# Half-size pieces of the conditioning weights in tiles of their own, and the scaling of the differential outputs on VectorE

## The chip, the cores and the metric

The kernel runs on one core of one Trainium2 chip. The metric is the device time of an execution in microseconds (us); smaller is better. Several runs are timed, and one execution per kernel is recorded by the hardware profiler, from which every duration here comes. Engine names are those of the profile: PE is TensorE (PEld its weight load), DVE is VectorE, ACT is ScalarE, POOL is GpSimd, and SP is the engine that issues most of the loads.

## What is computed

One layer of a diffusion backbone, in fp32, over 256 latent and 256 context tokens with 2048 channels. Cut to what matters here:

```
m_lat = split(silu(c)     @ w_ada + b_ada, 6)          # shift, scale, gate, ... each of 2048
m_ctx = split(silu(c_ctx) @ w_ada + b_ada, 6)
hc = rms_norm(ctx, norm1_g) * (1 + m_ctx[1]) + m_ctx[0]
h  = rms_norm(x,   norm1_g) * (1 + m_lat[1]) + m_lat[0]
ka, va, kb, vb = split(hc @ w_in[:, :KV]), split(h @ w_in[:, :KV])   # keys and values, both streams
qa, qb, ga, gb = split(h @ w_in[:, KV:])                             # queries and gates, latent only
oa = gqa(rope(norm(qa)), ka, va)                       # 16 heads of 128
a  = softmax(q1 k1) - lam * softmax(q2 k2)             # differential attention, 8 heads
ob = rms_norm(a @ vb, subln_g) * (1 - lam_init)
x  = x + m_lat[2] * ((sig(ga) * (oa @ w_br_a) + sig(gb) * (ob @ w_br_b)) @ w_out)
out = x + gate * swiglu(modulated norm of x)           # with w_ff_gate, w_ff_up, w_ff_down
```

## The kernel before

Every large product is made in three matmuls, because fp32 operands are split into a high and a low part. Weights come in tiles of 512 KB (two k-tiles of 128 by 512 columns; `load_w`, DMA at L224) into the pool tag "wraw" of 7 buffers. ACT casts a tile to its high part (`whi`, L235), DVE subtracts that from the tile for the low part (`wlo`, L237), and TensorE then does high x high, high x low and low x high (L241, L242, L243 in `mm3`). All these loads stand in the queue of SP, one behind the other: a DMA that must wait for its tile to become free holds up every one behind it.

The first stage makes keys and values. It walks over the 16 k-tiles in steps (first k-tile, number of k-tiles): (0,1), (1,1), (2,2), (4,4), (8,4), (12,4). In each step, `kv_group` multiplies six column groups of weights with the modulated tokens of that step (`xT` latent, `cT` context) and adds the result to accumulators on DVE (L442) or ACT.

Before a step can start, `ada_cond(k0, nk)` must have made its shift and scale: two parts (shift, then scale), each a product of the conditioning vectors (`cst`) with 16 k-tiles of columns of the conditioning weights `ada_t`. These come in pieces, each of 512 KB: for steps of four k-tiles 8 pieces a part, of two k-tiles each. Each part is 16 matmuls (L314; in fp32 a row of the profile counts 32 records), and its pieces are named `wada`. The pieces of a part go to different places: for all steps of four, the first two go to the halves of one large tile (L299), the next two are loaded as half-size pieces of 256 KB (L303), each into a scratch tile, one with the tag "nr" (2 buffers) and one with the tag "p" (4 buffers); the last four go to wraw tiles (L294). All 16 matmuls of a part run as one group, in reverse order of the pieces. After it a copy, a transposition (`atp`, L324) and small DVE operations make shift and scale, and `modulated` turns the tokens `tok_t` (loaded at L170) into `xT` and `cT` (L356 to L360 on DVE and ACT).

The generator yields inside `ada_cond` and the others mark where work of different kinds is interleaved; the order within an engine follows from the order in which the program issues, and the scheduler keeps an issued order where `tc.issue_after` asks for it.

The rotary tables are made on POOL by `tables` (L198): 32 small multiplications from the loaded tiles `cs` and `used`, which have the tag "p" too. In the first stage ACT and DVE also serve the next conditioning values (`ada` on DVE, L457 and L459, from loads `wada` at L452).

In the attention stage (about 390 to 620 us in the profile), the units of the differential attention come in 16 calls. For each, TensorE makes the output `o` (L835), ACT copies it to SBUF (`on`, L836), makes its sum of squares (L839), DVE scales the sum to a mean (`rstdo`, L123), POOL takes the power -1/2 (L124), and ACT scales `on` by it (L842). One generator step later TensorE transposes it (`otp`, L845), and ACT writes it out (L846). Between these stand the casts and subtractions of weights for the query and gate columns.

Of the kernel before, what the change touches and what calls it, by code (L numbers as in the profile page):

```python
# [11 lines left out]
F32 = mybir.dt.float32  # L12
# [5 lines left out]
P = 128  # L18
# [28 lines left out]
def hybrid_block(ctx: ExitStack, tc: tile.TileContext, t: dict, out: bass.AP):  # L47
# [161 lines left out]
        nc.vector.tensor_scalar(out=neglam, in0=neglam, scalar1=-LAM_INIT, scalar2=None, op0=ALU.add)  # L209


    last_hi, last_lo = [], []

    def load_raw(r0, c0, n=2):
        raw = wp.tile([P, WK, CG], F32, tag="wraw", bufs=WRAW, name="wraw")
# [5 lines left out]

    def load_w(src, r0, c0, nk=WK, in_big=False):
        raw = wp.tile([P, WK, CG], F32, tag="wraw", bufs=WRAW, name="wraw")
        nc.sync.dma_start(out=raw[:, 0:nk], in_=src[r0:r0 + nk * P, c0:c0 + CG].rearrange("(k p) c -> p k c", p=P))  # L224
        return split_w(raw, nk, in_big)

    def split_w(raw, nk, in_big=False, late=None):
# [52 lines left out]
    def ada_cond(k0, nk):  # L280
        ncol = nk * P
        kk = 2 * CG // ncol
        n0 = k0 * P * 2 * D // (P * 2 * CG)
        mod = []
        for part in range(2):
            aps = s_ps("ada")
            held = []
            for q in range(0, NKT, kk):
                piece = t["ada_t"][n0].rearrange("p (k c) -> p k c", c=ncol)
                n0 += 1  # L290
                n = q // kk
                if nk < 4 or n > 3:
                    wt = wp.tile([P, 2 * CG], F32, tag="wraw", bufs=WRAW, name="wada").rearrange("p (k c) -> p k c", c=ncol)
                    nc.sync.dma_start(out=wt, in_=piece)  # L294
                elif n < 2:
                    if n == 0:
                        two = big_tile("wada2").rearrange("p (n k c) -> p n k c", n=2, c=ncol)
                    wt = two[:, n]
                    nc.sync.dma_start(out=wt, in_=piece)  # L299
                else:  # L300
                    wt = [scratch("wada1", tag=tag, bufs=b) for tag, b in (("nr", 2), ("p", 4))]
                    for j in range(2):
                        nc.sync.dma_start(out=wt[j], in_=piece[:, j, :])  # L303
                held += [(q + j, wt[j] if nk == 4 and 1 < n < 4 else wt[:, j, :]) for j in range(kk)]
                last = q + kk == NKT
                if k0 and not last:
                    if nk == 4 and n == 3:
                        yield None
                    continue
                for k, rhs in held[::-1] if k0 else held:  # L310
                    g = k % 4
                    early, late_k = k < 4, k >= NKT - 4
                    with tc.issue_after(last_pe[0].ins) if k0 == 1 and k == held[-1][0] else nullcontext():
                        last_pe[0] = nc.tensor.matmul(aps[32 * g:32 * g + 32, 0:ncol], lhsT=cst[:, k, :], rhs=rhs,  # L314
                                                      start=late_k if k0 else early, stop=early if k0 else late_k)
                held = []
                if last:
                    asb = scratch("asb")
                    last_asb.append(nc.scalar.copy(out=asb[:, 0:ncol], in_=aps[:, 0:ncol]))
                yield None  # L320
                if last:
                    atp = tp_ps("atp")
                    for j in range(nk):
                        nc.tensor.transpose(out=atp[:, j * P:(j + 1) * P], in_=asb[:, j * P:(j + 1) * P], identity=ident)  # L324
                    m = small(f"mod{part}", 8)
                    mv = m[:, 0:2 * nk].rearrange("p (j w) -> p j w", w=2)
                    nc.vector.tensor_reduce(
                        out=mv, in_=atp[:, 0:ncol].rearrange("p (j g m) -> p j m g", g=4, m=32)[:, :, 0:2, :],
                        axis=AX.X, op=ALU.add)
                    nc.vector.tensor_tensor(out=mv, in0=mv,  # L330
                                            in1=bada[:, part * NKT + k0: part * NKT + k0 + nk].unsqueeze(2).to_broadcast([P, nk, 2]), op=ALU.add)
                    mod.append(mv)
        shift, scale = mod
        nc.vector.scalar_tensor_tensor(out=scale, in0=scale, scalar=1.0,
                                       in1=g1[:, k0:k0 + nk].unsqueeze(2).to_broadcast([P, nk, 2]), op0=ALU.add, op1=ALU.mult)
        cond_of[k0] = (shift, scale)
# [465 lines left out]
    def back(br, u, pr):  # L802

        grp, hh = unit(br, u)
        if br == "a":
            if hh % 2 == 0:
                pair[:] = [big_tile("pT", F32R).rearrange("p (k c) -> p k c", k=4) for _ in range(2)]
            pT = list(pair)
        else:
            pT = scratch("pT", tag="pTb", bufs=2).rearrange("p (k c) -> p k c", k=4)  # L810
        for i, p in enumerate(pr):
            tp = tp_ps("ptp")
            for kt in range(4):
                nc.tensor.transpose(out=tp[:, kt * P:(kt + 1) * P], in_=p[:, kt * P:(kt + 1) * P], identity=ident)  # L814
            src = tp.rearrange("p (k q) -> p k q", k=4)
            if br == "a":
                c0 = hh % 2 * SEQ + i * P
                split(*[x[:, :, c0:c0 + P] for x in pT], src)
            else:
                nc.scalar.copy(out=pT, in_=src)  # L820
        yield None
        if br == "a" and hh % 2 == 0:
            return
        op = tp_ps("o")
        if br == "a":
            for kt in range(4):
                vh, vl = [v[:, kt, grp * AD:(grp + 1) * AD] for v in v_a]
                mm3(op, vh, vl, pT[0][:, kt, :], pT[1][:, kt, :], kt == 0, kt == 3)
            last_o.append(nc.scalar.copy(out=o_raw(grp * 4 + hh - 1, 2), in_=op))
            return  # L830
        vb = acc["vb"][grp].rearrange("p (t c) -> p t c", c=CG)
        tk = u % 2
        on = scratch("on", BV, tag="on", bufs=2)
        for kt in range(4):
            nc.tensor.matmul(op[:, 0:BV], lhsT=pT[:, kt, :], rhs=vb[:, kt, hh * BV:(hh + 1) * BV], start=(kt == 0), stop=(kt == 3))  # L835
        nc.scalar.copy(out=on, in_=op[:, 0:BV])  # L836
        junk = scratch("junk_o", tag="sq", bufs=2)
        ss = small("sso", 1)
        nc.scalar.activation(out=junk[:, 0:BV], in_=on, func=AF.Square, accum_out=ss)  # L839
        r = rstd_of(ss, 1, BV, "rstdo")  # L840
        yield None
        nc.scalar.mul(out=on, in_=on, mul=r)  # L842
        yield None
        tp = tp_ps("otp")
        nc.tensor.transpose(out=tp[:, 0:P], in_=on, identity=ident)  # L845
        nc.scalar.mul(out=o_raw(AH + grp * 4 + hh)[:, tk * P:(tk + 1) * P], in_=tp[:, 0:P], mul=gsub)  # L846
# [335 lines left out]
```

## Time and profile before

| | |
|---|---|
| median of 3 runs | 1704.09 us (1702.79 to 1705.93) |
| the profiled execution | 1703.83 us, span 1701.7 us |
| clock granted to TensorE, mean | 0.997 |
| TensorE busy | 1676.8 us, 99% of the span |
| DVE, ACT, POOL busy | 67%, 46%, 12% |
| DMA | 413.08 MB, 243 GB/s on average |

How to read it: a row of a timeline has the start in us, the duration, the engine, the line, the operation, output <- input, and in brackets for how long the engine was idle before it and which engine's instruction (with its line) ended the wait. Matmuls are pipelined: the distance of their starts counts, not their length. A row of the windows has the window, its length, the busy time and the number of instructions of PE, PEld, DVE, ACT and POOL, then the clock granted to TensorE (1.00 is full speed), the share of DMA and GB/s. In the waits, the numbers are the total in us, how many times, and the longest. In the chain of waits a row has start, length and what ran; "SPq" is the issue of a DMA by SP. A row for one line has the shortest, median and longest duration in ns, and the first and last start.

### The profile page before, as it was taken

The page shows a single profiled execution, that of the slowest core. Times are in us where ns is not written, and L with a number is a line of the kernel's source. Part 1 is how long each engine was busy: PE and PEld are TensorE (multiplying, and loading weights), DVE is VectorE, ACT ScalarE, POOL GpSimd, SP SyncE. Part 2 cuts the span into 40 slices and gives each one's busy share as a digit, 9 for nine tenths or more (in the row PEclk, how much of TensorE's full clock was granted, in tenths as well). Part 3 has the DMA queues.
Part 4 walks back from the last instruction along what each step waited for, and adds up shares of the span by engine and source line. Part 5 has one row for each costly group of instructions (what it writes and reads, how often), then busy time and mean ns, then how long its engine had stood idle before and what let it go on. Part 6 is the DMA issues. An engine that isn't in the chain of part 4 may idle for free.

```text
span 1701.7 us, 21519 instructions
## 1 busy us (share of the span) xinstructions
PE 1676.8 (99%) x7889; PEld 1355.1 (80%) x7889; DVE 1138.4 (67%) x1438; ACT 779.0 (46%) x1071; POOL 209.3 (12%) x296
## 2 busy tenths in 40 slices
PE   7999999999999999999999999999999999999998
PEld 5677778887887778888888888888888888888887
DVE  5665779798687878996666755566666666554454
ACT  5221222246666656577544534444444444333332
POOL 0200002011231210011111101111111111100000
PEclk9999999999999999999999999999999999999999
DMA  9787875778766768776777857788888888766662
GB/s 352 288 316 275 304 253 157 234 252 256 246 180 216 222 225 272 246 238 212 256 265 237 294 175 221 235 263 267 263 272 263 269 274 253 238 218 195 216 207 88
DMA packets 181860, 413.08 MB, mean 243 GB/s; under 512 B 15065, under 2 KB 16298, under 8 KB 181498
## 3 DMA queue, kind: packets, MB, share of 16 engines
q1 hardware_dynamic: 169482, 374.17, 67.3%
q0 software_dynamic: 12272, 37.53, 7.4%
q8 instruction: 62, 1.02, 0.3%
q14 instruction: 44, 0.36, 0.1%
HBM read 395.35 MB, written 16.29 MB: 242 GB/s over the span
## 4 chain that ended last, share of the span: by engine, by line
PE 75%; issue 10%; DVE 6%; DMA 4%; POOL 3%; ACT 2%; SPq 0%; POOLq 0%; DVEq 0%; ACTq 0%
PE mm L241 22%; PE mm L242 22%; PE mm L243 22%; DVE wlo L237 2%; PE ada L314 1%; POOL fturn L1091 1%; ACT whi L235 1%; PE ptp L814 1%; DMA turn_d<-fpart 1%; DMA fturn<-turn_d 1%; DMA wraw<-in_w_in_dram 1%; DVE ada L459 1%; PE mm L401 1%; PE o L835 1%; DVE mx L736 1%
## 5 line engine op out<-in xcount | busy, mean ns | idle before, releaser
L237 DVE TENSOR_TENSOR wlo<-wraw,whi 128x1024 fp32r<-128x1024 f32 x498 | 606.8, 1220 | 443.9 <-ACT whi L235 442.9
L235 ACT CAST whi<-wraw 128x1024 fp32r<-128x1024 f32 x498 | 522.4, 1050 | 714.0 <-PE mm L243 607.2
L242 PE MATMUL mm<-wlo,hT 128*128 128x512 f32 x684 | 266.3, 389 | 0.1
L243 PE MATMUL mm<-whi,hT 128*128 128x512 f32 x684 | 266.1, 389 | 0.0
L241 PE MATMUL mm<-whi,hT 128*128 128x512 f32 x684 | 266.1, 389 | 0.0
L241 PE MATMUL mm<-whi,xT 128*128 128x512 f32 x630 | 252.7, 402 | 1.3 <-ACT xT L359 1.2
L242 PE MATMUL mm<-wlo,xT 128*128 128x512 f32 x630 | 247.0, 392 | 4.3 <-DVE wlo L237 4.3
L243 PE MATMUL mm<-whi,xT 128*128 128x512 f32 x630 | 246.9, 392 | 0.0
L459 DVE SCALAR_TENSOR_TENSOR ada<-wada,vt,ada 128x1024 f32<-128x1024 f32 x120 | 152.0, 1277 | 0.0
L242 PEld LDWEIGHTS mm<-wlo,hT 128*128 128x128 f32 x684 | 128.4, 188 | 27.7 <-DVE wlo L237 0.9
L241 PEld LDWEIGHTS mm<-whi,hT 128*128 128x128 f32 x684 | 128.4, 188 | 26.7
L243 PEld LDWEIGHTS mm<-whi,hT 128*128 128x128 f32 x684 | 128.4, 188 | 26.5
L241 PEld LDWEIGHTS mm<-whi,xT 128*128 128x128 f32 x630 | 118.6, 188 | 32.7 <-issue 7.0
L242 PEld LDWEIGHTS mm<-wlo,xT 128*128 128x128 f32 x630 | 118.8, 189 | 28.2 <-DVE wlo L237 5.7
L243 PEld LDWEIGHTS mm<-whi,xT 128*128 128x128 f32 x630 | 118.5, 188 | 26.0 <-DVE xT L360 0.3
L241 PE MATMUL mm<-whi,fT 128*128 128x512 f32 x354 | 137.5, 388 | 0.5 <-DVE y L1127 0.5
L242 PE MATMUL mm<-wlo,fT 128*128 128x512 f32 x354 | 137.3, 388 | 0.0
L243 PE MATMUL mm<-whi,fT 128*128 128x512 f32 x354 | 137.3, 388 | 0.0
L241 PEld LDWEIGHTS mm<-whi,fT 128*128 128x128 f32 x354 | 66.4, 188 | 15.0 <-issue 0.8
L243 PEld LDWEIGHTS mm<-whi,fT 128*128 128x128 f32 x354 | 66.5, 188 | 13.8
L242 PEld LDWEIGHTS mm<-wlo,fT 128*128 128x128 f32 x354 | 66.4, 188 | 13.7
L241 PE MATMUL mm<-whi,oT 128*128 128x512 f32 x192 | 75.9, 396 | 0.0
(236 smaller groups left out, 2150.4 us busy)
## 6 DMA issues: line engine op xcount, KB each, us to landing
wraw<-in_w_in_dram SPq DMA_DIRECT2D x159, 512.0 KB, 4.7
wada<-in_w_ada_dram SPq DMA_DIRECT2D x128, 512.0 KB, 4.6
wraw<-in_w_ff_gate_dram SPq DMA_DIRECT2D x88, 512.0 KB, 4.6
wraw<-in_w_ff_up_dram SPq DMA_DIRECT2D x88, 512.0 KB, 5.4
wraw<-in_w_ff_down_dram SPq DMA_DIRECT2D x88, 512.0 KB, 4.8
wada<-in_ada_t_dram SPq DMA_DIRECT2D x52, 512.0 KB, 7.8
wraw<-in_w_br_a_dram SPq DMA_DIRECT2D x32, 512.0 KB, 5.3
wraw<-in_w_out_dram SPq DMA_DIRECT2D x32, 512.0 KB, 5.2
```

What stands on the lines that cost most here:

```text
L235: last_hi.append(nc.scalar.copy(out=hi[:, 0:nk], in_=raw[:, 0:nk]))
L237: last_lo.append(nc.vector.tensor_tensor(out=lo[:, 0:nk], in0=raw[:, 0:nk], in1=hi[:, 0:nk].bitcast(F32), op=ALU.subtract))
L241: nc.tensor.matmul(ps, lhsT=ah, rhs=wh, start=first, stop=False, skip_group_check=skip)
L242: nc.tensor.matmul(ps, lhsT=ah, rhs=wl, start=False, stop=False, skip_group_check=skip)
L243: return nc.tensor.matmul(ps, lhsT=al, rhs=wh, start=False, stop=last, skip_group_check=skip)
L314: last_pe[0] = nc.tensor.matmul(aps[32 * g:32 * g + 32, 0:ncol], lhsT=cst[:, k, :], rhs=rhs, start=late_k if k0 else early, stop=early if ...
L401: last_pe[0] = nc.tensor.matmul(ps[cg], lhsT=x, rhs=ws0[cg][y], start=(n == 0), stop=(n == 2))
L459: nc.vector.scalar_tensor_tensor(out=dst, in0=wt, scalar=sc[:, 0, kt:kt + 1], in1=dst, op0=ALU.mult, op1=ALU.add)
L736: nc.vector.tensor_reduce(out=mx, in_=sp, axis=AX.X, op=ALU.max, negate=True)
L814: nc.tensor.transpose(out=tp[:, kt * P:(kt + 1) * P], in_=p[:, kt * P:(kt + 1) * P], identity=ident)
L835: nc.tensor.matmul(op[:, 0:BV], lhsT=pT[:, kt, :], rhs=vb[:, kt, hh * BV:(hh + 1) * BV], start=(kt == 0), stop=(kt == 3))
L1091: nc.gpsimd.dma_start(out=whole[32 * b:32 * b + 32].rearrange("p (k a j) -> p k a j", k=4, a=4), in_=blocks[b])
```

## The change

Three things are changed. First, in step (4,4) all eight pieces of a part go to wraw tiles, and its 16 matmuls run as two groups: the pieces of the first half (k-tiles 0 to 7) as soon as they are there, those of the second half behind them. Second, in steps (8,4) and (12,4) the half-size pieces go to scratch tiles with the tags "nr" twice, "sq" and "pTb" (2 buffers each), and no longer to "p"; the DMAs of all pieces of these steps are ordered behind the last weights' load issued before. That is an order, not a wait for the load to land. Third, the scaling of `on` is a tensor_scalar of DVE (L843 of the changed kernel) and no longer an activation of ACT (L842). From L314 on, line numbers of the changed kernel are one higher.

```diff
-    last_hi, last_lo = [], []
+    last_hi, last_lo, last_load = [], [], []
...
     def load_w(src, r0, c0, nk=WK, in_big=False):
...
-        nc.sync.dma_start(out=raw[:, 0:nk], in_=src[r0:r0 + nk * P, c0:c0 + CG].rearrange("(k p) c -> p k c", p=P))
+        last_load.append(nc.sync.dma_start(out=raw[:, 0:nk], in_=src[r0:r0 + nk * P, c0:c0 + CG].rearrange("(k p) c -> p k c", p=P)))
...
-                if nk < 4 or n > 3:
-                    wt = wp.tile([P, 2 * CG], F32, tag="wraw", bufs=WRAW, name="wada").rearrange("p (k c) -> p k c", c=ncol)
-                    nc.sync.dma_start(out=wt, in_=piece)
...
-                else:
-                    wt = [scratch("wada1", tag=tag, bufs=b) for tag, b in (("nr", 2), ("p", 4))]
-                    for j in range(2):
-                        nc.sync.dma_start(out=wt[j], in_=piece[:, j, :])
-                held += [(q + j, wt[j] if nk == 4 and 1 < n < 4 else wt[:, j, :]) for j in range(kk)]
+                with tc.issue_after(last_load[-1].ins) if k0 >= 8 else nullcontext():
+                    if k0 < 8 or n > 3:
+                        wt = wp.tile([P, 2 * CG], F32, tag="wraw", bufs=WRAW, name="wada").rearrange("p (k c) -> p k c", c=ncol)
+                        nc.sync.dma_start(out=wt, in_=piece)
...
+                    else:
+                        wt = [scratch("wada1", tag=tag, bufs=2) for tag in (("nr", "nr") if n == 2 else ("sq", "pTb"))]
+                        for j in range(2):
+                            nc.sync.dma_start(out=wt[j], in_=piece[:, j, :])
+                held += [(q + j, wt[j] if k0 >= 8 and 1 < n < 4 else wt[:, j, :]) for j in range(kk)]
                 last = q + kk == NKT
-                if k0 and not last:
-                    if nk == 4 and n == 3:
+                if k0 and not last and (k0 != 4 or n != 3):
+                    if k0 >= 8 and n == 3:
                         yield None
                     continue
...
-        nc.scalar.mul(out=on, in_=on, mul=r)
+        nc.vector.tensor_scalar(out=on, in0=on, scalar1=r, scalar2=None, op0=ALU.mult)
```

How the order on the engines moves is shown at three places. The first is SP's queue around the pieces of step (4,4); `wada` by L294 (L295 of the changed kernel) are full pieces in wraw tiles, those by L303 half-size pieces, `wraw` are weights. Before:

```order
L224 DMA wraw<-in_w_in_dram 128x2x512
L294 DMA wada<-in_ada_t_dram 128x1024
L303 DMA wada_860<-in_ada_t_dram 128x512
L294 DMA wada<-in_ada_t_dram 128x1024 x3
L224 DMA wraw<-in_w_in_dram 128x2x512
L170 DMA tok_t_686<-in_x_t_dram 128x1024
```

In the changed kernel:

```order
L224 DMA wraw<-in_w_in_dram 128x2x512
L295 DMA wada<-in_ada_t_dram 128x1024 x4
L224 DMA wraw<-in_w_in_dram 128x2x512
L295 DMA wada<-in_ada_t_dram 128x1024
L170 DMA tok_t_686<-in_x_t_dram 128x1024
```

The half-size piece of part 1 in front of the weights and the tokens (`tok_t`) is gone; the first four pieces of part 0 and one of its second half stand there as full ones.

The second place is TensorE's order around the ada matmuls of part 0 of step (4,4), which run during step (2,2). Before, all 16 stand behind the last matmuls of a column group:

```order
L242 MATMUL mm<-wlo,cT 128x512
L243 MATMUL mm<-whi,cT 128x512
L314 MATMUL ada<-wada,cst 32x512 x8
L314 MATMUL ada<-wada_742,cst 32x512
L314 MATMUL ada<-wada_741,cst 32x512
L314 MATMUL ada<-wada_738,cst 32x512
L314 MATMUL ada<-wada_737,cst 32x512
L314 MATMUL ada<-wada_734,cst 32x512 x4
L241 MATMUL mm<-whi,xT_207 128x512
```

In the changed kernel, at the end of the column group two groups ahead:

```order
L242 MATMUL mm<-wlo,cT 128x512
L243 MATMUL mm<-whi,cT 128x512
L315 MATMUL ada<-wada,cst 32x512 x4
L241 MATMUL mm<-whi,xT_207 128x512
L242 MATMUL mm<-wlo,xT_207 128x512
```

Four now stand 48 matmuls earlier, four more 24 matmuls earlier, and the last eight where all 16 were; behind those eight the first two matmuls of the next group are both L241, which need only the cast.

The third place is DVE's order in one of the 16 units of the differential attention (`rstdo` is the unit's mean, `on` its output, `mx` the maximum of the scores of another). Before:

```order
L237 TENSOR_TENSOR wlo<-wraw,whi 128x1024
L123 TENSOR_SCALAR rstdo<-sso 128x1
L459 SCALAR_TENSOR_TENSOR ada_2770<-wada_4950,vt,ada_2770 128x1024
L237 TENSOR_TENSOR wlo<-wraw,whi 128x1024
L736 TENSOR_REDUCE mx<-s 128x1
```

In the changed kernel:

```order
L237 TENSOR_TENSOR wlo<-wraw,whi 128x1024
L123 TENSOR_SCALAR rstdo<-sso 128x1
L460 SCALAR_TENSOR_TENSOR ada_2764<-wada_4944,vt,ada_2764 128x1024
L843 TENSOR_SCALAR on<-on,rstdo 128x128
L237 TENSOR_TENSOR wlo<-wraw,whi 128x1024
L737 TENSOR_REDUCE mx<-s 128x1
```

The scaling stands ahead of a subtraction of weights. In most units one or more operations stand between the mean and the scaling; in four of the 16 the scaling follows it directly.

One more place is told in words. In part 1 of step (12,4), SP's order of before is weights, a conditioning load (L452), weights, two half-size pieces; the other two of this part come much earlier. In the changed kernel all four half-size pieces stand behind the conditioning load and ahead of those second weights. They use the tiles that part 0 held, and so wait for matmuls of part 0's ada group. From about 640 us on the order of all engines is the same in both kernels.

More of the change, by code (lines that the diff above doesn't have):

```diff
@@ L291, in ada_cond @@
                 n = q // kk
-                if nk < 4 or n > 3:
-                    wt = wp.tile([P, 2 * CG], F32, tag="wraw", bufs=WRAW, name="wada").rearrange("p (k c) -> p k c", c=ncol)
-                    nc.sync.dma_start(out=wt, in_=piece)
[L295 to L299, printed above, removed]
-                else:
-                    wt = [scratch("wada1", tag=tag, bufs=b) for tag, b in (("nr", 2), ("p", 4))]
-                    for j in range(2):
-                        nc.sync.dma_start(out=wt[j], in_=piece[:, j, :])
@@ L304, in ada_cond @@
-                held += [(q + j, wt[j] if nk == 4 and 1 < n < 4 else wt[:, j, :]) for j in range(kk)]
+                with tc.issue_after(last_load[-1].ins) if k0 >= 8 else nullcontext():
+                    if k0 < 8 or n > 3:
+                        wt = wp.tile([P, 2 * CG], F32, tag="wraw", bufs=WRAW, name="wada").rearrange("p (k c) -> p k c", c=ncol)
+                        nc.sync.dma_start(out=wt, in_=piece)
+                    elif n < 2:
+                        if n == 0:
+                            two = big_tile("wada2").rearrange("p (n k c) -> p n k c", n=2, c=ncol)
+                        wt = two[:, n]
+                        nc.sync.dma_start(out=wt, in_=piece)
+                    else:
+                        wt = [scratch("wada1", tag=tag, bufs=2) for tag in (("nr", "nr") if n == 2 else ("sq", "pTb"))]
+                        for j in range(2):
+                            nc.sync.dma_start(out=wt[j], in_=piece[:, j, :])
@@ L305, in ada_cond @@
+                held += [(q + j, wt[j] if k0 >= 8 and 1 < n < 4 else wt[:, j, :]) for j in range(kk)]
                 last = q + kk == NKT
-                if k0 and not last:
-                    if nk == 4 and n == 3:
+                if k0 and not last and (k0 != 4 or n != 3):
+                    if k0 >= 8 and n == 3:
                         yield None
                     continue
+                first_ks, last_ks = (range(0, 4), range(12, 16)) if k0 == 0 else (range(4, 8), range(8, 12)) if k0 == 4 else (range(12, 16), range(0, 4))
@@ L310, in ada_cond @@
                 for k, rhs in held[::-1] if k0 else held:
                     g = k % 4
-                    early, late_k = k < 4, k >= NKT - 4
                     with tc.issue_after(last_pe[0].ins) if k0 == 1 and k == held[-1][0] else nullcontext():
                         last_pe[0] = nc.tensor.matmul(aps[32 * g:32 * g + 32, 0:ncol], lhsT=cst[:, k, :], rhs=rhs,
-                                                      start=late_k if k0 else early, stop=early if k0 else late_k)
+                                                      start=k in first_ks, stop=k in last_ks)
```

## The prediction

> **What bounds the kernel now.** I read the page first: its busy times and the share of each engine.
>
> ```profile
> span 1701.7 us, 21519 instructions
> PE 1676.8 (99%) x7889; PEld 1355.1 (80%) x7889; DVE 1138.4 (67%) x1438; ACT 779.0 (46%) x1071; POOL 209.3 (12%) x296
> ```
>
> TensorE is busy for 1676.8 of 1701.7 us and no matmul is taken away, so the change can win only the 24.9 us in which TensorE stands still, and the time in which it runs at a lower clock. The profiled execution took 1703.83 us, the span and 2.13 us around it; that is 0.26 us under the median of 1704.09, so a sum made against it needs no correction. About 0.2% (3.4 us) is what a measurement of this kernel can tell from no change. Next I asked for the waits of TensorE, and for the windows in which the idle time lies.
>
> ```profile
> PE mm L242 <- DVE wlo L237: 4.3, 2, 3.0
> PE mm L241 <- DVE kb L442: 2.7, 1, 2.7
> PE mm L241 <- ACT xT L359: 1.2, 1, 1.2
> ...
> PE o L835 <- DVE kaT L247: 0.6, 1, 0.6
> ```
>
> ```profile
> 60.00:80.00 20.00, 16.13 (x71) 11.38 (x73) 11.71 (x23) 3.02 (x6) 1.78 (x9) 0.91 0.86 325
> 500.00:600.00 100.00, 96.30 (x483) 75.14 (x483) 81.97 (x132) 62.52 (x124) 20.09 (x18) 0.98 0.70 222
> ```
>
> Two places carry most of what lies between start and end: 3.9 us idle at a clock of 0.91 around 70 us, and 3.7 us idle at 0.98 between 500 and 600. The change reaches both. The first is explained by the chain of waits.
>
> ```profile
> 60.09 1.70 POOL rp_kb L198 x8
> ...
> 61.81 0.33 SPq L303
> ...
> 63.68 7.04 DMA wraw<-in_w_in_dram
> ...
> 70.83 1.05 ACT whi L235
> ...
> 71.90 1.23 DVE wlo L237
> ```
>
> SP stands at a half-size piece (L303) until POOL has made the last rotary table (rp_kb) at 61.79. POOL reads the tables' inputs from tiles with the tag "p", and the half-size piece wants such a tile. Everything behind it in SP's queue is late, the weights of 63.68 too; they land 7.04 us later and pass through cast and subtraction. TensorE's timeline shows both ends of it, and a window the clock behind it (the last but two of its columns).
>
> ```profile
> 56.33 1.93 PE L314 MATMUL ada<-wada,cst 128*32 128x256 f32 x32
> ...
> 61.05 0.39 PE L243 MATMUL mm<-whi,cT 128*128 128x512 f32 x1
> 62.66 0.50 PE L241 MATMUL mm<-whi,xT 128*128 128x512 f32 x1 [1.22 <-ACT xT L359]
> ...
> 70.75 0.39 PE L243 MATMUL mm<-whi,xT 128*128 128x512 f32 x1
> 73.79 0.50 PE L241 MATMUL mm<-whi,cT 128*128 128x512 f32 x1 [2.65 <-DVE kb L442]
> ...
> 78.32 3.64 PE L314 MATMUL ada<-wada,cst 128*32 128x512 f32 x32
> 81.89 0.50 PE L241 MATMUL mm<-whi,xT 128*128 128x512 f32 x1
> ```
>
> ```profile
> 74.00:76.00 2.00, 2.00 (x6) 1.57 (x6) 1.52 (x3) 0.00 (x0) 0.00 (x0) 0.55 1.03 416
> ```
>
> From 62.66 to 81.89 stand 48 matmuls and one ada group. The 36 matmuls from 62.66 to 70.75 are 35 steps of 0.23 us, the first of them longer; at 0.228 a step 48 take 10.9 us, and the group 81.89 - 78.32 = 3.6. That is 14.5 of 19.2 us, so 4.7 are lost: 2.8 by the wait (70.75 to 73.79 less a step), and 1.9 by the clock of 0.55 behind it.
>
> The Trainium skill (TensorE: Matmul & The Clock Gate, Part 1) has the clock halve after at least one idle window of about 3.4 us, and the window runs freely. This trace differs: 2.65 us of idle were followed by 0.55. By the page alone the lower clock would not hang on this wait, and the sum below would be 1.9 us worse; the row decides.
>
> **Step (4,4) in weights' tiles.** All pieces of this step now take wraw tiles, which POOL never reads. What is late next is the ada group of the step before, whose matmuls give the tiles back from 56.33 us on: an estimate by quarters of its 1.93 us puts the third and fourth piece of part 0 on SP at 56.9 and 57.4, and the weights behind them at 57.9 instead of 63.68. The first four ada matmuls of part 0 now stand where TensorE had its hole of 1.22 us, and need the piece of 57.4. For a full-size load onto an idle queue the nearest rows, of the issues between 48 and 82 us, are these (the last number is the time to landing):
>
> ```profile
> wada<-in_ada_t_dram SPq DMA_DIRECT2D x9, 512.0 KB, 8.1
> ...
> wada<-in_ada_t_dram SPq DMA_DIRECT2D x5, 256.0 KB, 3.3
> ```
>
> Half the size lands in 3.3 us, the full size in a filled queue in 8.1. Two loads on an empty queue are nearer to the former; I take 5.2, so TensorE starts these four at 62.6. They and the rest of the same 14.5 us bring it to 77.1, where before had 81.89: **-4.8 us**. If the piece lands in 3.3 us, the activation behind the hole (62.66) holds the next matmul, the four lie in the hole, and TensorE is at 62.66 + 14.5 - 0.9 = 76.3: -5.6. If it takes 8.1, TensorE starts at 65.5 and wins 1.9. Two small new waits stand against this. The next weights but one wait on SP for a subtraction until about 68.4; 7.04 us to land and 2.3 of cast and subtraction make them ready at 77.7, for a matmul at 77.1 or soon behind: 0.1, since two matmuls that need only the cast are put first there. And one accumulation on VectorE now stands behind the modulation: 0.25. **Sum -4.45**, from -5.6 to -1.55.
>
> **Steps (8,4) and (12,4).** The half-size pieces move to tags that are used in later stages, and behind a weights' load on SP. In part 1 of the last step they wait for part 0's ada group, and now the weights behind them wait too. TensorE, SP and ACT there:
>
> ```profile
> 198.79 3.64 PE L314 MATMUL ada<-wada,cst 128*32 128x512 f32 x32
> ...
> 213.26 0.39 PE L243 MATMUL mm<-whi,cT 128*128 128x512 f32 x1
> ```
>
> ```profile
> 199.89 0.38 SPq L224 DMA_DIRECT2D wraw<-in_w_in_dram  x1
> ```
>
> ```profile
> 206.55 1.05 ACT L235 CAST whi<-wraw 128x1024 fp32r<-128x1024 f32 x1 [3.10 <-DMA wraw<-in_w_in_dram]
> ```
>
> Before, these weights are issued at 199.89 and cast 6.66 us later; their subtraction is needed near 213.3. Now four half pieces go first, which wait for about two thirds of the group (201.3) and take some 0.4 us each: issue 203.2, cast 209.9, subtraction done by 212.2. One us of cover is left, so **0**. With the 8.1 us of the row above, the stall is 0.3; with two more loads of 1.1 us in front, 2.5.
>
> **VectorE's scaling (L842).** 16 activations leave ACT, and 16 tensor_scalar of the same 128x128 come to DVE. The nearest operation of that form on DVE, then what the means' tile (rstdo) shows:
>
> ```profile
> L146 DVE TENSOR_SCALAR tok<-tok,sums x4: 285/286/288, 9.9 to 29.0; 128x128 f32<-128x128 f32 x4
> ```
>
> ```profile
> L124 POOL TENSOR_TENSOR rstdo<-rstdo,neghalf x16: 548/1456/3204, 395.4 to 614.6; 128x1 f32<-128x1 f32 x16
> L842 ACT ACTIVATE on<-on,rstdo x16: 402/403/407, 397.5 to 616.2; 128x128 f32<-128x128 f32 x16
> ...
>   POOL rstdo L124: 33.0, 16
> ```
>
> DVE gains 16 x 0.29 = 4.6 us of work and ACT loses 6.4, all beside TensorE. What matters is who stands still for POOL: ACT does for 33.0 us, and the cast (whi) behind it stands too. DVE waits for that cast 30 times; then DVE and ACT at 554 to 558:
>
> ```profile
> DVE wlo L237 <- ACT whi L235: 30.6, 30, 2.7
> ```
>
> ```profile
> 554.65 1.27 DVE L459 SCALAR_TENSOR_TENSOR ada<-wada,vt,ada 128x1024 f32<-128x1024 f32 x1
> 557.74 1.22 DVE L237 TENSOR_TENSOR wlo<-wraw,whi 128x1024 fp32r<-128x1024 f32 x1 [1.82 <-ACT whi L235]
> ```
>
> ```profile
> 556.37 0.40 ACT L842 ACTIVATE on<-on,rstdo 128x128 f32<-128x128 f32 x1 [2.36 <-POOL rstdo L124]
> 556.67 1.03 ACT L235 CAST whi<-wraw 128x1024 fp32r<-128x1024 f32 x1
> ```
>
> Now DVE waits from 555.9 to 556.37 for POOL, scales for 0.29 and subtracts at 556.66, since the cast has run before: 1.08 us earlier than 557.74. Queued behind the waiting DVE are that subtraction and the maxima of the scores; TensorE feels them only where its lead is gone, and that is here, with the clock behind the first:
>
> ```profile
> 574.93 0.50 PE L242 MATMUL mm<-wlo,xT 128*128 128x512 f32 x1 [2.98 <-DVE wlo L237]
> ...
> 636.58 0.50 PE L242 MATMUL mm<-wlo,xT 128*128 128x512 f32 x1 [1.29 <-DVE wlo L237]
> ```
>
> ```profile
> 576.00:578.00 2.00, 2.00 (x6) 1.61 (x5) 2.00 (x5) 0.00 (x0) 1.58 (x1) 0.50 0.74 254
> 578.00:580.00 2.00, 2.00 (x9) 0.94 (x8) 1.21 (x2) 0.34 (x2) 1.62 (x1) 0.66 0.54 159
> ```
>
> If the 1.08 us carry through from 557 to 574.93, less 0.25 for the next scaling among DVE's work, 2.98 becomes 2.15: **-0.83**; if nothing does, +0.25. I take the gain, as DVE's idle time is mostly for the cast. At 636 the last scaling lies 20 us back: -0.3, between 0 and -0.66 (estimates, parts of the same 1.08). The wait of 0.6 us for kaT grows by 0.1 (0 to one scaling, 0.3). **Sum -1.0**, from -1.5 to +0.55.
>
> All together -4.45 - 1.0 = -5.45: 1703.83 - 5.45 = **1698.4 us**, by the terms' bounds 1696.7 to 1702.8.
>
> **The rivals.** *The clock stays up at 574 (larger gain).* The two windows lose 0.50 and 0.34 of 2 us each, 1.7. If the wait falls clearly under the 2.65 us that lowered the clock at 73.79, this goes as well: 1696.7. For: 2.15 is under both waits that were followed by it. Against: the rows say only that 1.29 didn't lower it, not where the limit lies.
>
> *The gain is given back near 213, or the pieces land late (no change that can be told).* A stall of 2.5 us there with the clock loss of 1.9 gives 1702.8; pieces that take 8.1 us give 1701.3. For: eight pieces and the weights go in a burst. Against: the cast had 3.10 us of idle ahead of it.
>
> *VectorE's wait for POOL reaches TensorE (slower).* DVE works in order; 16 times it may stand for the pow (median 1.46) and scale for 0.29: 28 us. If a third reaches TensorE, 9.3 us, the sum is +3.85: 1707.7. It decides from 5.45 us on. For: in four units the scaling stands right behind its own mean. Against: before, the cast stood behind the same POOL for 33.0 us, and TensorE lost some 5.
>
> The Trainium skill (SBUF — State Buffer, Who interferes with whom) says that POOL and a VectorE operation with two SBUF operands shut each other out for a whole instruction, so the pow would be short once VectorE waits for it. The trace agrees with 548 ns at the shortest beside a median of 1456. By it the rival's 28 us were 16 x (0.55 + 0.29) = 13.4, and the case 1702.9.
>
> *The change doesn't do what it says*: SP waits as long for other tiles, and attention's 1.0 alone is left: 1702.8.
>
> **How the numbers follow.** The forecast has 0.48, the larger gain 0.17, given back or late 0.22, slower 0.09, no effect 0.04. The time is the forecast's, 1698.4. From 1695.5 (the larger gain, with 1.2 of the terms' bounds) to 1702.8 the range leaves out the slower case and about 0.1 at the edges. Faster by over 3.4 us (under 1700.4): the forecast but for 0.02, the larger gain, and 0.05 of the late cases, 0.68. Slower 0.09, the same 0.23.
>
> **What would show it.** DMA goes on between 58 and 62 us; the wait of 2.65 us and the half clock behind it are gone; the matmul behind all of part 0's ada is at about 77. No wait over 1 us stands at 205 to 215. ACT's 33.0 us for POOL are gone, DVE has 16 waits of mostly under 1 us, and the 2.98 are near 2.1. It would be wrong with a wait over 2 us for wada at 62, for wlo at 208 to 214, or several new ones for wlo between 395 and 620.

## The result and the profile after

The changed kernel takes 1693.7 us (median of 6 runs, 1692.2 to 1696.49) against 1703.44 us of before (6 runs, 1700.08 to 1705.93). The ratio is 0.9947 with a 95% interval of 0.9932 to 0.9961, so it is faster by 9.0 us (6.6 to 11.6). Forecast were 1698.4 us, a gain of 5.45, and a range that ended at 1695.5: the sign was right, the gain too small by two fifths. The profiled execution of the changed kernel took 1696.49 us, the longest of its six, with a span of 1694.7.

The page, and the waits of TensorE:

```profile
span 1694.7 us, 21499 instructions
```

```profile
PE ada L315 <- DMA wada<-in_ada_t_dram: 6.0, 2, 5.3
PE mm L242 <- DVE wlo L237: 3.1, 4, 1.9
```

The 2.7 us for kb (L442), the 1.2 for xT and the 0.6 for kaT are gone from this list; the longest wait for wlo is 1.9 and not 3.0. SP's queue and TensorE around step (4,4):

```profile
45.61 12.51 SPq L295 DMA_DIRECT2D wada<-in_ada_t_dram  x4
58.22 0.38 SPq L224 DMA_DIRECT2D wraw<-in_w_in_dram  x1
```

```profile
61.35 0.39 PE L243 MATMUL mm<-whi,cT 128*128 128x512 f32 x1
62.45 1.06 PE L315 MATMUL ada<-wada,cst 128*32 128x512 f32 x8 [0.72 <-DMA wada<-in_ada_t_dram]
63.45 0.50 PE L241 MATMUL mm<-whi,xT 128*128 128x512 f32 x1
...
69.11 1.06 PE L315 MATMUL ada<-wada,cst 128*32 128x512 f32 x8
...
75.78 1.92 PE L315 MATMUL ada<-wada,cst 128*32 128x512 f32 x16
77.63 0.74 PE L241 MATMUL mm<-whi,xT 128*128 128x512 f32 x2
```

SP issues these weights at 58.22 where before it was 63.68. The first four ada matmuls (8 records) begin at 62.45 and lie in what was the hole. From there nothing waits up to the matmul behind all of this part's ada, which starts at 77.63; in before it started at 81.89. The window of 60 to 80 us shows the clock at 1.00, where before had 0.91:

```profile
60.00:80.00 20.00, 19.28 (x98) 12.69 (x97) 13.63 (x26) 4.40 (x7) 0.71 (x4) 1.00 0.85 328
```

In attention, DVE from one unit's mean to the next one's, and the means' tile with the scaling:

```profile
546.89 0.15 DVE L123 TENSOR_SCALAR rstdo<-sso 128x1 f32<-128x1 f32 x1
546.95 1.27 DVE L460 SCALAR_TENSOR_TENSOR ada<-wada,vt,ada 128x1024 f32<-128x1024 f32 x1
548.67 0.29 DVE L843 TENSOR_SCALAR on<-on,rstdo 128x128 f32<-128x128 f32 x1 [0.44 <-POOL rstdo L124]
548.87 1.22 DVE L237 TENSOR_TENSOR wlo<-wraw,whi 128x1024 fp32r<-128x1024 f32 x1
...
557.61 0.15 DVE L123 TENSOR_SCALAR rstdo<-sso 128x1 f32<-128x1 f32 x1
```

```profile
L843 DVE TENSOR_SCALAR on<-on,rstdo x16: 266/287/290, 392.7 to 608.1; 128x128 f32<-128x128 f32 x16
...
  POOL rstdo L124: 7.0, 13
```

The subtraction follows the scaling without a gap. ScalarE's 33.0 us of waiting for the power have become 7.0 us of VectorE's. TensorE there:

```profile
571.77 0.50 PE L242 MATMUL mm<-wlo,xT 128*128 128x512 f32 x1 [0.56 <-DVE wlo L237]
```

```profile
628.05 0.50 PE L242 MATMUL mm<-wlo,xT 128*128 128x512 f32 x1 [1.86 <-DVE wlo L237]
```

The matmul that waited 2.98 us before (574.93) doesn't wait now; 0.56 us is left one group later. The wait that was 1.29 us at 636.58 has become 1.86 at 628.05.

The profiled pair adds up like this. At 77.63 the changed kernel is 4.26 us ahead; it was 0.29 late at 56.3, so step (4,4) wins 4.55. Attention wins the 0.61 of kaT, 2.98 - 0.56, and the half clock behind the long wait, 1.7, and loses 0.57 at 628: 4.2. With the 4.26 that is 8.5, which is what lies between 636.58 and 628.05. Half clock follows the 1.86 us too and costs 1.7; at the end of the spans 7.0 is left.

### The profile page after: what moved, and what is told of

Read it like the earlier page. It is cut to its first block, busy times and chain, and to the rows that moved or that the text cites. A ratio compares the mean times of both kernels' runs of the same rounds, so it can differ in the third digit from the quotient of the medians.

```text
span 1694.7 us, 21499 instructions
## 1 busy us (share of the span) xinstructions
PE 1675.7 (99%) x7889; PEld 1354.8 (80%) x7889; DVE 1143.0 (67%) x1454; ACT 776.4 (46%) x1055; POOL 202.3 (12%) x296
## 4 chain that ended last, share of the span: by engine, by line
PE 92%; DVE 3%; DMA 2%; ACT 1%; issue 1%; POOL 0%; SPq 0%; DVEq 0%; ACTq 0%; POOLq 0%
PE mm L242 28%; PE mm L241 28%; PE mm L243 28%; PE ada L315 2%; PE ptp L815 1%; DVE wlo L237 1%; PE s L791 1%; PE mm L402 1%; PE o L836 1%; DMA wada<-in_ada_t_dram 1%; DMA wraw<-in_w_ff_gate_dram 0%; ACT whi L235 0%; DMA gate_d<-gate 0%; DMA wraw<-in_w_in_dram 0%; DVE ada L460 0%
## 5 line engine op out<-in xcount | busy, mean ns | idle before, releaser
L241 PE MATMUL mm<-whi,hT 128*128 128x512 f32 x684 | 266.1, 389 | 0.0
L241 PE MATMUL mm<-whi,xT 128*128 128x512 f32 x630 | 251.9, 402 | 0.0
L241 PEld LDWEIGHTS mm<-whi,hT 128*128 128x128 f32 x684 | 128.4, 188 | 26.8
L241 PEld LDWEIGHTS mm<-whi,xT 128*128 128x128 f32 x630 | 118.2, 188 | 33.0 <-issue 6.6
L241 PE MATMUL mm<-whi,fT 128*128 128x512 f32 x354 | 137.5, 388 | 0.5 <-DVE y L1128 0.5
L241 PEld LDWEIGHTS mm<-whi,fT 128*128 128x128 f32 x354 | 66.4, 188 | 15.0 <-issue 0.8
L241 PE MATMUL mm<-whi,oT 128*128 128x512 f32 x192 | 75.9, 396 | 0.0
```

The costliest lines, as they stand in the source:

```text
L241: nc.tensor.matmul(ps, lhsT=ah, rhs=wh, start=first, stop=False, skip_group_check=skip)
```

## Experiments

Each kernel's ratio was measured against runs of the kernel before on the same chip; gains and losses below are that ratio by 1702 us.

**The two halves of the change.** First all but the scaling (`e1_kv`):

```diff
-        nc.vector.tensor_scalar(out=on, in0=on, scalar1=r, scalar2=None, op0=ALU.mult)
+        nc.scalar.mul(out=on, in_=on, mul=r)
```

> All of the change but the scaling on VectorE, which goes back to ScalarE (whole layer computed). Theory (the change's gain has two independent halves: the conditioning loads about 4.3 us, the scaling the rest): 3.5 to 5.0 us under before, the wait of some 3 us for wlo near 570 us stays (2.5 to 3.2) with half clock behind it. Rival (the wait near 570 went because TensorE and the loads arrive there 4 us earlier, not by the scaling): 8 to 10 us under before, that wait under 1 us.

Measured: 1699.38 us, ratio 0.9982 (0.9973 to 0.9991), 3.1 us faster (1.5 to 4.6), a little less than the 3.5 to 5.0 that were expected. TensorE's wait stays where the theory had it:

```profile
571.06 0.79 PE L242 MATMUL mm<-wlo,xT 128*128 128x512 f32 x1 [2.92 <-DVE wlo L237]
```

Then the scaling alone (`e2_scale`), on the kernel before:

```diff
-        nc.scalar.mul(out=on, in_=on, mul=r)
+        nc.vector.tensor_scalar(out=on, in0=on, scalar1=r, scalar2=None, op0=ALU.mult)
```

> Only the scaling on VectorE; the conditioning loads as before (whole layer computed). Theory: 3.5 to 5.5 us under before; the wait near 575 us falls from 2.98 to 0.3 to 0.9 and no half clock follows it; the wait of 2.65 us at 73.8 stays. The size that was predicted, one unit's shift of 0.83: the wait at 575 is 2.0 to 2.3 and the gain is about 1 us. Rival (scaling without the earlier loads brings nothing): within 1 us of before.

Measured: 1697.02 us, ratio 0.9968 (0.9956 to 0.998), 5.4 us faster (3.4 to 7.5).

```profile
73.22 0.50 PE L241 MATMUL mm<-whi,cT 128*128 128x512 f32 x1 [2.32 <-DVE kb L442]
...
574.77 0.50 PE L242 MATMUL mm<-wlo,xT 128*128 128x512 f32 x1 [0.52 <-DVE wlo L237]
```

The early wait stays, the late one falls to 0.52. As far as the intervals tell, the halves are independent: 3.1 + 5.4 = 8.5 beside the 9.0 of the whole. The scaling, which was forecast as the smaller half (1.0), is the larger.

**How many units of the scaling it takes.** The changed kernel with only unit 11 on VectorE (`e6_one`), and with units 9 to 11 (`e7_three`):

```diff
-        nc.vector.tensor_scalar(out=on, in0=on, scalar1=r, scalar2=None, op0=ALU.mult)
+        if u == 11:          # e7_three: 9 <= u <= 11
+            nc.vector.tensor_scalar(out=on, in0=on, scalar1=r, scalar2=None, op0=ALU.mult)
+        else:
+            nc.scalar.mul(out=on, in_=on, mul=r)
```

> The changed kernel with the scaling on VectorE in one unit of 16 only, the one before the last ahead of the wait near 570 us (unit 11); ScalarE scales the other 15 (whole layer computed). Theory (each unit on VectorE brings the subtractions about 0.8 to 1.1 us forward, and the units add up while the stretch isn't bound by TensorE): the wait near 570 is 1.7 to 2.4 us. Rival (one unit right ahead is all that counts): under 1 us.

> The same with units 9, 10 and 11 on VectorE. Theory (the units add up): the wait near 570 is 0 to 1.1 us, no half clock behind it, time within 1.5 us of the changed kernel. Rival (one unit is all that counts): the same wait as with unit 11 alone. Rival (all units since 390 us are needed): 1.5 us or more of the wait left.

Measured: 1699.16 us (ratio 0.9979, 0.9969 to 0.9989) and 1696.98 us (0.9959, 0.9946 to 0.9973). TensorE's wait near 570 with one unit:

```profile
569.17 0.50 PE L242 MATMUL mm<-wlo,xT 128*128 128x512 f32 x1 [1.66 <-DVE wlo L237]
```

With three units this wait is gone; of the whole list for wlo this is left, with the longest at 629.86 us:

```profile
PE mm L242 <- DVE wlo L237: 1.8, 3, 1.3
```

No unit 2.92 (e1_kv), one 1.66, three none: the units add up, the first by 1.26 us, the three by 2.92 or more. One alone lies just under its range (1.7 to 2.4). The rival with one unit as all that counts falls.

What is added up can be read from the starts of the means (`rstdo`) on VectorE and of the output (`o`) on TensorE. Four units of before:

```profile
519.79 0.14 DVE L123 TENSOR_SCALAR rstdo<-sso 128x1 f32<-128x1 f32 x1
...
566.03 0.15 DVE L123 TENSOR_SCALAR rstdo<-sso 128x1 f32<-128x1 f32 x1
```

```profile
527.76 1.05 PE L835 MATMUL o<-vb,pT 128*128 128x128 f32 x8
...
570.66 1.05 PE L835 MATMUL o<-vb,pT 128*128 128x128 f32 x8
```

In the changed kernel VectorE's four units begin with this row and end with the one at 557.61 above:

```profile
514.36 0.14 DVE L123 TENSOR_SCALAR rstdo<-sso 128x1 f32<-128x1 f32 x1
```

TensorE takes 42.9 us for four units, in the changed kernel too (522.30 to 565.21). VectorE takes 46.2 before and in e1_kv, 44.9 with one unit, 43.3 with three and in the changed kernel: the steps of 1.3 and 2.9 are those of the wait. The time of e7_three doesn't quite follow its wait: by the ratios it is 2.0 us over the changed kernel, where at most 1.5 was expected, but the intervals overlap. Its TensorE still has waits of 0.62 us for kaT (513.6) and 0.71 for qT (579.8), which the changed kernel doesn't have.

**Which part of the conditioning edits is needed.** Only the half-size pieces' tags on the kernel before (`e5_tags`):

```diff
-                    wt = [scratch("wada1", tag=tag, bufs=b) for tag, b in (("nr", 2), ("p", 4))]
+                    wt = [scratch("wada1", tag=tag, bufs=2) for tag in (("nr", "nr") if n == 2 else ("sq", "pTb"))]
```

> Only the tags of the half-size pieces: nr twice, sq and pTb instead of nr and p, in all three steps of four; the step (4,4) keeps its half pieces and its group of 16, no order behind the weights' load, scaling on ScalarE (whole layer computed). Theory (the wait for GpSimd's tables alone held the queue): no standstill of SP to 61.8 us, the wait of 2.65 us at 73.8 and the half clock behind it gone, 4 to 5 us under before; the hole of 1.2 us at 62 stays. Rival (the first four ada matmuls in the hole and the full-size pieces are needed too): a wait of over 1 us remains between 62 and 90, gain under 3 us.

Measured: 1704.18 us, ratio 1.0011 (1.0002 to 1.002): 1.9 us slower (0.3 to 3.4). SP no longer stands for POOL, and the weights go at 59.27:

```profile
50.85 8.33 SPq L294 DMA_DIRECT2D wada<-in_ada_t_dram  x4
59.27 0.90 SPq L224 DMA_DIRECT2D wraw<-in_w_in_dram  x2
```

```profile
65.31 1.93 PE L314 MATMUL ada<-wada,cst 128*32 128x512 f32 x6 [3.49 <-DMA wada<-in_ada_t_dram]
...
68.19 0.63 PE L241 MATMUL mm<-whi,xT 128*128 128x512 f32 x1
68.61 0.63 PE L243 MATMUL mm<-whi,xT 128*128 128x512 f32 x1
```

My theory fell here: the wait for POOL did go, and another took its place. Without the pieces held back, three ada matmuls (6 records) come to stand in TensorE's hole, but run from the last piece backwards, and that one lands late: 3.49 us of waiting, and matmuls 0.42 us apart behind it instead of 0.23. Then step (4,4) alone (`e11_step4`), and the later steps alone (`e12_later`):

```diff
# e11_step4: the changed kernel with the scaling on ScalarE, and
-                with tc.issue_after(last_load[-1].ins) if k0 >= 8 else nullcontext():
+                with nullcontext():
...
-                        wt = [scratch("wada1", tag=tag, bufs=2) for tag in (("nr", "nr") if n == 2 else ("sq", "pTb"))]
+                        wt = [scratch("wada1", tag=tag, bufs=b) for tag, b in (("nr", 2), ("p", 4))]
```

> Of the change only step (4,4): full-size pieces in weights' tiles and two groups of 8; the later steps with the tags nr and p and without the order, scaling on ScalarE (whole layer computed). Theory (the whole gain of the conditioning part is the filled hole and the earlier queue of step (4,4)): 2.5 to 4.5 us under before, as with all of that part. Rival (the later steps' tags are needed, their half-size pieces meet a busy tile elsewhere): under 1.5 us.

```diff
# e12_later: the kernel before, with
+                with tc.issue_after(last_load[-1].ins) if k0 >= 8 else nullcontext():
...
-                    wt = [scratch("wada1", tag=tag, bufs=b) for tag, b in (("nr", 2), ("p", 4))]
+                        wt = [scratch("wada1", tag=tag, bufs=b) for tag, b in ((("nr", 2), ("p", 4)) if k0 < 8 else (("nr", 2), ("nr", 2)) if n == 2 else (("sq", 2), ("pTb", 2)))]
```

> Of the change only steps (8,4) and (12,4): half-size pieces with the tags nr, sq and pTb, ordered behind the weights' load; step (4,4) as before, scaling on ScalarE (whole layer computed). Theory (in before the piece that stands still for GpSimd is one of step (4,4), so this alone changes nothing): within 1 us of before, the waits at 62 and 73.8 us as before. Rival (the later steps carry part of the gain): 1.5 to 3 us under before.

Measured: e11_step4 1705.64 us, ratio 1.002 (1.001 to 1.0031), 3.4 us slower; e12_later 1702.56 us, ratio 1.0003 (0.9994 to 1.0012), no change, with both waits as before (1.18 and 3.05 us). SP and TensorE of e11_step4:

```profile
48.68 12.16 SPq L304 DMA_DIRECT2D wada<-in_ada_t_dram  x5
60.94 0.85 SPq L295 DMA_DIRECT2D wada<-in_ada_t_dram  x2
61.88 0.38 SPq L224 DMA_DIRECT2D wraw<-in_w_in_dram  x1
```

```profile
66.73 1.93 PE L315 MATMUL ada<-wada,cst 128*32 128x512 f32 x8 [5.45 <-DMA wada<-in_ada_t_dram]
```

The theory for e11_step4 fell too. The half-size pieces of the later steps (L304), which nothing holds back now, have moved ahead of two pieces of step (4,4). Of the 12.16 us in which SP issues five of them, 9.1 are one wait for POOL's last rotary table (rp_kb), as in before. Neither half gains anything alone. Which of the two edits of the later steps protects the first? The changed kernel without the order (`e14_noorder`), and without the tags (`e15_oldtags`):

```diff
# e14_noorder
-                with tc.issue_after(last_load[-1].ins) if k0 >= 8 else nullcontext():
+                with nullcontext():
# e15_oldtags
-                        wt = [scratch("wada1", tag=tag, bufs=2) for tag in (("nr", "nr") if n == 2 else ("sq", "pTb"))]
+                        wt = [scratch("wada1", tag=tag, bufs=b) for tag, b in (("nr", 2), ("p", 4))]
```

> The changed kernel without the order behind the weights' loads; the new tags and everything else stay (whole layer computed). In SP's program four half-size pieces of the step after stand again ahead of the third piece of step (4,4). Theory (the order is what keeps them away; their loads, 1 MB, delay the pieces that TensorE's hole needs by 1 to 3 us): a wait of 1.5 to 4 us for wada at 62 us instead of 0.7, 1 to 5 us over the changed kernel. Rival (tags alone suffice, since these tiles don't wait for GpSimd): within 1 us of the changed kernel.

> The changed kernel with the old tags nr and p for the half-size pieces of the later steps; the order behind the weights' loads and everything else stay (whole layer computed). Theory (the order is what counts for TensorE, and by 77 us GpSimd's tables are long done): within 1.2 us of the changed kernel. Rival (tag p meets its readers again): 2 to 5 us over it, with a wait between 90 and 230 us.

Measured: e14_noorder 1695.56 us (ratio 0.9958, 0.9945 to 0.9972), e15_oldtags 1694.68 us (0.9958, 0.9946 to 0.9971). SP and TensorE of e14_noorder:

```profile
48.83 2.49 SPq L304 DMA_DIRECT2D wada<-in_ada_t_dram  x4
57.06 0.92 SPq L295 DMA_DIRECT2D wada<-in_ada_t_dram  x2
```

```profile
63.35 1.06 PE L315 MATMUL ada<-wada,cst 128*32 128x512 f32 x8 [1.88 <-DMA wada<-in_ada_t_dram]
```

Four pieces of the later step are in front again, but with their new tags they don't stand, and TensorE's hole is 1.88 us where the changed kernel's is 0.72. So either edit alone keeps SP from standing for POOL. That the pieces in front cause the longer wait isn't shown by this: e15_oldtags has 2.07 us at the same place, and there SP issues in the same order as in the changed kernel and the loads landed later in this execution (7.4 us at the median of the eight pieces between 44 and 66 us, 6.6 in the changed kernel). By the ratios both lie 0.5 to 1.9 us above the changed kernel (0.9947, and 0.9955 in the later run e10_after), with intervals that overlap: what each edit is worth beside the other stays open. Open as well is what the two groups of eight matmuls add to the earlier queue, as no run has the full-size pieces with one group of 16.

**The clock.** 20 transposes of the identity in the wait at 73.8 us of the kernel before (`e9_fill_before`), 14 ahead of the one at 628 us of the changed kernel (`e8_fill_after`); nobody reads them:

```diff
+                idle = tp_ps("idle")
+                with tc.issue_after(end.ins):
+                    for _ in range(20):
+                        still = nc.tensor.transpose(out=idle[:, 0:P], in_=ident, identity=ident)
```

> The kernel before, with 20 transposes of the identity (nobody reads them) in TensorE's wait of 2.65 us at 73.8; everything else as before. Theory (the clock halves because TensorE idles over half of a fixed window of 3.4 us): the wait for kb stays in place as a shorter one (0.2 to 0.8 us idle), matmuls behind it follow after 0.23 us, 1.5 to 2.0 us under before. Rival (the clock falls for another reason than idle time): matmuls after 0.43 us as before, no gain.

> The changed kernel with 14 transposes of the identity (nobody reads them) right ahead of TensorE's wait of 1.86 us at 628 us. Theory (idle time over half of a window halves the clock, and where the window's edges fall decides): no half clock at 628 to 632, 0.5 to 1.7 us under the changed kernel on average, the spread of its times smaller. Rival (that half clock is chance and not set by the wait): times as the changed kernel, half clock there in some runs.

Measured: e9_fill_before 1701.23 us, ratio 0.9995 (0.9986 to 1.0004); e8_fill_after 1694.58 us (1693.75 to 1695.22), ratio 0.9947 (0.9935 to 0.9959). Three waits of e9_fill_before:

```profile
74.04 0.50 PE L241 MATMUL mm<-whi,cT 128*128 128x512 f32 x1 [0.43 <-DVE kb L449]
```

```profile
572.69 0.50 PE L242 MATMUL mm<-wlo,xT 128*128 128x512 f32 x1 [2.95 <-DVE wlo L237]
```

```profile
635.02 0.50 PE L242 MATMUL mm<-wlo,xT 128*128 128x512 f32 x1 [1.84 <-DVE wlo L237]
```

The filled wait isn't followed by half clock (first row below), as the theory says. But the wait of 2.95 us at 572.69 isn't either, although 2.92 us in e1_kv was, while 1.84 us at 635.02 is. The traces hold a pattern that fits both. They record when the granted clock changed, and in all 16 profiled executions every stretch of half clock begins a whole number of steps of 3.413 us after the first record of that execution. Cut along these steps, the last two waits and the windows behind them are:

```profile
76.00:78.00 2.00, 2.00 (x17) 0.96 (x19) 1.11 (x2) 0.00 (x0) 0.00 (x0) 1.00 1.01 397
```

```profile
570.87:574.29 3.42, 1.60 (x7) 1.34 (x8) 3.42 (x8) 2.48 (x6) 1.13 (x2) 1.00 0.14 23
574.29:577.70 3.41, 3.41 (x20) 2.31 (x19) 3.41 (x5) 0.29 (x1) 3.09 (x1) 1.00 0.69 220
632.31:635.73 3.42, 1.58 (x7) 1.00 (x6) 3.42 (x6) 0.59 (x1) 0.23 (x1) 1.00 0.40 92
635.73:639.14 3.41, 3.41 (x10) 2.63 (x9) 3.31 (x3) 0.00 (x0) 0.00 (x0) 0.50 0.84 255
```

A window's edge cuts the 2.95 us into 1.13 and 1.82, while the 1.84 us lie in one window: TensorE stands still for 53% of the one window and 54% of the other, and only the second is followed by half clock. The time of the whole execution doesn't show the fill's gain: it is 0.9 us less than before by the ratio, between 2.4 less and 0.7 more, so the expected 1.5 to 2.0 us are neither shown nor excluded. The same holds for e8_fill_after: its trace has no half clock ahead of the program's end, but its time can't be told from the changed kernel's, where 0.5 to 1.7 us less was expected.

**The scaling on GpSimd** (`e4_pool`, and again beside the changed kernel, `e13_pool` and `e10_after`):

```diff
-        nc.vector.tensor_scalar(out=on, in0=on, scalar1=r, scalar2=None, op0=ALU.mult)
+        nc.gpsimd.tensor_scalar(out=on, in0=on, scalar1=r, scalar2=None, op0=ALU.mult)
```

> The changed kernel with the scaling on GpSimd, behind its power in the same queue; neither ScalarE nor VectorE waits for it (whole layer computed). Theory (what counts is that the cast's and the subtraction's engine stands still for GpSimd): the 7.0 us of VectorE's waits go, the times are 0 to 2 us under the changed kernel. Rival (GpSimd is slow at it or shuts VectorE out, and TensorE's transposition waits): 1 to 5 us over the changed kernel, with new waits at the transposition of on.

> The changed kernel with the scaling on GpSimd, again, on the chip of the run beside it. Theory (no engine that TensorE depends on stands still for the power): 1 to 3 us under the changed kernel, no wait over 1 us between 500 and 640. Rival (the earlier difference was the chip's): within 0.8 us of the changed kernel.

> The changed kernel once more, beside the version with the scaling on GpSimd on the same chip. Expected 8 to 10.5 us under before. Theory (the mean of 10 us holds, and the wait at 628 lowers the clock in some runs only): times spread over 3 to 5 us. Rival (the gain was overstated by the runs so far): 5.5 us, as predicted.

Measured: e4_pool 1691.68 us (1690.96 to 1692.8), ratio 0.993 (0.9918 to 0.9943). On one chip then e13_pool 1692.81 us (1691.63 to 1693.38), ratio 0.9947 (0.9935 to 0.996), and e10_after 1693.76 us (1693.4 to 1695.26), ratio 0.9955 (0.9941 to 0.9969): the five runs of each don't overlap (by 0.02 us), but 0.95 us is about a tenth of the whole gain, and the intervals of the ratios overlap. So the 1 to 3 us that were expected are not shown. e10_after itself is 7.7 us faster than before (5.3 to 10.0), where 8 to 10.5 was expected, and its times spread over 1.9 us and not 3 to 5. The tile `on` of e13_pool, and the only wait of its TensorE between 500 and 640 us:

```profile
L843 POOL TENSOR_SCALAR on<-on,rstdo x16: 607/614/1707, 392.8 to 606.4; 128x128 f32<-128x128 f32 x16
```

```profile
625.62 0.50 PE L242 MATMUL mm<-wlo,xT 128*128 128x512 f32 x1 [0.66 <-DVE wlo L237]
```

GpSimd takes 0.61 us for what VectorE does in 0.29, but TensorE's transposition of `on` never waits for it. The wait of 1.86 us at 628 is 0.66, and the 0.56 at 572 is gone. This version had the lowest median on both chips.

## Why the prediction was too small

**What bounds the kernel** held: the two places named carry the gain, and from 640 us on the pair differs by little but the half clock at 629.

**Step (4,4) in weights' tiles** (-4.45 forecast) was right in its mechanism: the pieces go at 57 to 58 us, the four matmuls start at 62.45 (62.6 forecast), TensorE is at 77.63 (77.1 and 0.35 of small waits forecast), 4.55 us in the profiled pair. Over all runs it is 3.1 us, between 1.5 and 4.6 (e1_kv). A likely reason for the difference, not shown, are the 1.9 us of clock that the sum counted in full: the profiled execution of before had a mean clock of 0.997, and its other runs lie between 0.996 and 1.000, so that such losses are not in each of them. Beside the experiments before ran 69 times: the six runs at 0.996 have a median of 1704.3 us, the six at 1.000 one of 1700.9. The prediction let the pieces' tiles alone free the queue; e11_step4 shows that it needs the order or the tags of the later steps too.

**Steps (8,4) and (12,4)** (0 forecast): TensorE has no wait at 190 to 240 us, the cover held.

**VectorE's scaling** (-1.0 forecast) is the step that failed: "If the 1.08 us carry through from 557 to 574.93, less 0.25 for the next scaling among DVE's work, 2.98 becomes 2.15: -0.83". One unit's shift was sized a little low (1.08, or 0.83 after the next scaling; 1.26 with one unit, e6_one). What was wrong is that it was counted once. VectorE of before took 46.2 us for the four units up to 566 and TensorE needed 42.9: it fell behind by 0.8 us with each unit, until TensorE's lead was gone at 572. So every unit's shift counts, and three were enough for all of the 2.98 (e7_three). With the wait goes the half clock behind it, 1.7 us: what stood as the rival with the larger gain came true, with a wait that fell to 0.56 and not to 2.15, and the range ended too early. The wait for kaT, which was to grow by 0.1, is gone as well, another 0.6. The scaling alone measured 5.4 us (e2_scale) instead of 1.0. The forecast of -0.3 at 636 was wrong in its sign (+0.57 in the pair): TensorE gets there 9.1 us earlier (it stands from 626.19, before from 635.29), and VectorE's subtraction only 8.5.

**The rivals.** VectorE's wait for POOL (slower) has the form that was described, 13 waits of 7.0 us in all. None puts a new wait on TensorE; that something of it lies in the 0.56 and the 1.86 us is likely, as both shrink where the scaling is on GpSimd, but isn't separated from the scaling's own time. The power did not get short in all units, as the rule of the Trainium skill that was weighed there (SBUF — State Buffer, Who interferes with whom) would have it: its median is 1468 ns beside 1456 before. In both kernels it takes 0.55 to 0.57 us in six units and 1.4 or more in the other ten; in those VectorE runs operations with two operands beside it for most of that time, in most of them one that stands between the mean and the scaling.

## What to carry to other kernels

A wait at the end of a chain is worth the sum of what every round before it lost, not one round's loss: compare the rounds' period on the engines that wait for each other with what the bound engine needs, and look how far back the lag began. A queue's standstill is not cured by giving the standing load another tile if nothing holds the next one back: look what is hoisted into its place. An operation that must wait for a slow engine can stand behind it on that same engine, if nobody else needs that queue: here that was at least as fast, though the operation itself took twice as long.

## What the runs showed of the hardware

Half clock comes in stretches of 3.413 us, or twice that, and in each execution all of them begin on one grid of 3.413 us. By these traces, what decides is how much of one window of this grid TensorE stands still, not the length of the wait alone. Up to 700 us the 16 profiled executions have 14 such stretches. Each follows a window in which TensorE stood still for 53% or more of the time (1.80 us in e10_after is the least). A window with 50% or less was followed by none, unless it was at half clock itself, and one with 53% was not (the 1.82 us of e9_fill_before). So the limit lies near 53%, as far as these traces can place it; at the program's end, between other matmuls, 47% sufficed once (e1_kv). It follows that waits up to 1.67 us never had half clock behind them, that 1.84 us had it in e9_fill_before and not in e6_one (at 631 us, cut into 1.71 and 0.13), and that 2.95 us once had not. A second stretch came where the first itself began with 0.7 us or more of the same wait: after 2.92 (e1_kv), 3.49 (e5_tags) and 5.45 us (e11_step4), but not with 0.5 us (573.98 in e12_later). A single profile that shows such a stretch, or none, says little about the median. The Trainium skill (TensorE: Matmul & The Clock Gate, Part 1) has the window free-running, with which the grid agrees; its "after ≥1 idle window (~3.4µs)" does not agree, as little more than half of one sufficed.
